# Output projection of a two-layer decoder trunk: attention rows by seven products on half blocks, norm scale applied after the product

## The chip, the cores and the metric

The kernel runs on one core of a Trainium2 chip. The metric is device time in microseconds (us), the median of several executions. The core's engines run side by side, each working off its own queue in order: TensorE (PE; its weight loads are listed as PEld), VectorE (DVE), ScalarE (ACT), GpSimd (POOL) and the queue that issues DMAs (SP). They wait for each other through semaphores.

## The reference

Two layers, 256 tokens, model width 1024, all float32. Each layer computes

```python
h = rms_norm(x, ln_w);  proj = h @ w_in
q, k, v, g, z, xbc, dt = split(proj)
attn = moba_attention(q, k, v) * silu(g)             # 256 x 1024
y = ssd_scan(silu(conv(xbc)), dt) * silu(z)          # 256 x 1024
y = rms_norm(y.reshape(256, 2, 512), ssd_norm_w)     # two groups of 512
x = x + concat([attn, y]) @ w_out                    # w_out: 2048 x 1024
```

The change concerns the last two lines: the group norm and the product with `w_out`.

## The kernel before

Every float32 operand of a large product is split into a high part (a float32r copy, made by ACT) and a low part (the operand minus that copy, made by DVE). A product is three matmuls: high x high, low x high and high x low, all added in the same PSUM bank.

The weights lie in DRAM in the order of use, in pieces of 128 x 1024 float32 (512 KB). `Weights.load` fetches a piece into one of four `raw` buffers; `Weights.pump` turns it into a pair `wh` (ACT, L101) and `wl` (DVE, L102). There are eight such pairs (`NB`): a piece can be split once the pair eight places earlier has been read for the last time by TensorE. The pieces of layer 0 carry numbers: 48 to 55 are the z projection, 56 to 63 the attention rows of `w_out` (`oa0`, `oa1`), 64 to 71 its SSD rows (`ob`, `oc`). Layer 1 repeats the pattern.

A layer runs through the projections v, q, k, x, g, z and then the output projection. In g the attention output is gated into `aT` and split into `ah` and `al` (L189). In z the SSD output `x2` is gated (L510, L663), and after each half `group_norm` follows: squares (ACT), a sum over channels (L519), a one-column matmul `np` for the sum over partitions, a power on POOL, two diagonal matrices `dg` (L532), two float32 matmuls `rg` against ones that spread the scale over partitions (L537), the scaling of `x2` (L540, four instructions) and its split into `sh` and `sl` (L188, L189).

The output projection keeps four PSUM banks, one for each half of the tokens (t) and each half of the columns (j), and adds all sixteen row blocks of `w_out` into them: eight from attention, then two and six from SSD. A bank is 16 x 3 matmuls of 512 columns. Its end is one DVE addition to the residual `x` (L698); in layer 0 it is followed by the first steps of the next layer's norm, in layer 1 by the store.

A generator that has to wait for another engine is put aside and resumed after a number of weight pieces (`yield 3`). The order of each engine's instructions is set by the Tile framework when the program is built: it follows the program text, and a modelled timeline decides which ready instruction goes first. On the chip each engine keeps this order.

Of the kernel before, what the change touches and what calls it, by code (L numbers as in the profile page):

```python
# [15 lines left out]
P = 128  # L16
S = 256
# [31 lines left out]
class Weights:  # L49


    def __init__(self, nc, raw_pool, wh_pool, wl_pool, w):
        self.nc, self.w = nc, w
        self.raw_pool, self.wh_pool, self.wl_pool = raw_pool, wh_pool, wl_pool
        self.loads, self.subs, self.index = [], [], {}
        off = NX
        for l in range(NL):
            for name, _, kt, wd in CHUNKS:
                self.index[(l, name)] = len(self.subs)
                for r in range(kt // KR):  # L60
# [4 lines left out]
        self.nload = 0  # L65
        self.raw = {}
# [17 lines left out]
    def steps(i):  # L84

        return [slice(k, k + 1) for k in range(KR)] if i == 0 else [slice(0, KR)]

    def pump(self, upto=None, before=None):
        nc = self.nc
        upto = len(self.subs) if upto is None else upto  # L90
        while self.prepped < upto and self.prepped - self.freed < NB:
            i = self.prepped
            li, s, wd = self.subs[i]
            self.load(li + RAWB - 1)
            src = self.raw[li]
            h = self.wh_pool.tile([P, KS, 512], F32R, tag="wh", name=f"wh{i}")
# [7 lines left out]
            self.parts[i] = (h, lo)  # L104
            if s == KR // KS - 1:
                del self.raw[li]
            self.prepped += 1
# [14 lines left out]
def hybrid_kernel(ctx: ExitStack, tc: tile.TileContext, x, par, w, out):  # L122
# [188 lines left out]
    def first_norm(rs, hT, lT):  # L311

        dg = tmp.tile([P, S], F32, tag="sr", name="dg0", bufs=1)
        for t in range(2):
            tl = slice(t * P, (t + 1) * P)
            dve.tensor_scalar(dg[:, tl], ident, rs[:, t:t + 1], None, ALU.mult)
        yield 3
        rg = bank("rg0")
# [193 lines left out]

    def group_norm(L, g, y, sh, sl):
        pc = L * NPAR
# [11 lines left out]
        dve.tensor_scalar(nv, np_[:, 0:2], 1.0 / 512.0, 4.0 * EPS, ALU.mult, ALU.add)  # L526
        rn = small.tile([P, 2], F32, tag="rn", name="rn")
        rpow(rn, nv)
        dg = tmp.tile([P, S], F32, tag="sr", name="dg", bufs=1)
        for t in range(2):  # L530
            ts = slice(t * P, (t + 1) * P)
            dve.tensor_scalar(dg[:, ts], ident, rn[:, t:t + 1], None, ALU.mult)  # L532
        yield 2
        rg = bank("rg")
        for t in range(2):
            ts = slice(t * P, (t + 1) * P)
            pe.matmul(rg[:, ts], ones, dg[:, ts], start=True, stop=True)  # L537
        for c in range(4):
            ct = 4 * g + c
            dve.scalar_tensor_tensor(y[:, ct, :], y[:, ct, :],  # L540
                                     par_sb[:, pc + C_SW + ct:pc + C_SW + ct + 1], rg[:, 0:256],
                                     ALU.mult, ALU.mult)
            if c % 2:
                split(sh[:, ct - 1:ct + 1, :], sl[:, ct - 1:ct + 1, :], y[:, ct - 1:ct + 1, :])

    hT = lT = None
    msum = [None, None]
    for L in range(NL):
# [16 lines left out]
        else:  # L565
            hv, lv = hT, lT
            resume(pre_norm(L, 1, hT, lT, msum[1], 4))

# [76 lines left out]

        ah = keep.tile([P, 8, S], F32R, tag="qT", name=f"ah{L}")
        al = keep.tile([P, 8, S], F32R, tag="kT", name=f"al{L}")
# [10 lines left out]
        sl = keep.tile([P, 8, S], F32R, tag="cb1", name=f"sl{L}")  # L658
        for pr in range(4):
            ps = ps_p.tile([P, 512], F32, tag="ps_p", name=f"z{pr}")  # L660
# [3 lines left out]
            if pr % 2 == 1:  # L664
                resume(group_norm(L, pr // 2, x2, sh, sl))


        po = {}

        def mm_out(name, t, j, lh, ll, start, stop):  # L670
            for i, (c, ps) in enumerate(po[t, j]):
                mm_tokens(L, name, (t,), lh, ll, (ps,), start, stop,
                          t == 1 and i == len(po[t, j]) - 1, c)

        for j in range(2):
            for t in range(2):
                po[t, j] = [((0, 512), ps_p.tile([P, 512], F32, tag="ps_p", name=f"o{t}{j}"))]
                if L == NL - 1 and t == j == 1:

                    po[t, j] = [((0, 256), po[t, j][0][1]), ((256, 512), bank("o11b"))]  # L680
                mm_out(f"oa{j}", t, j, ah, al, True, False)
        drain()
        for j in range(2):
            for t in range(2):
                mm_out(f"ob{j}", t, j, sh, sl, False, False)
        region = tc.manual_schedule(engines={mybir.EngineType.PE})
        for t in range(2):
            msum[t] = small.tile([P, 2], F32, tag="ms", name=f"ms{t}")
            if t == 1:
                region.__enter__()  # L690
            for j in range(2):
                for i, ((a, b), ps) in enumerate(po[t, j]):
                    mm_tokens(L, f"oc{j}", (t,), sh, sl, (ps,), False, True,
                              t == 1 and b == 512, (a, b))
                    cs = slice(j * 512 + a, j * 512 + b)
                    xs = x_sb[t][:, cs]
                    with urgent():
                        dve.tensor_tensor(xs, xs, ps[:, a:b], ALU.add)  # L698
                    if L == NL - 1:
                        nc.sync.dma_start(out[t * P:(t + 1) * P, cs], xs)  # L700
                if L < NL - 1:
# [10 lines left out]
def layout(inputs):  # L712
# [56 lines left out]
```

## Time and profile before

| | |
|---|---|
| median of 3 runs | 453.02 us (452.85 to 453.19) |
| the profiled execution | 452.3 us, span of its instructions 450.5 us |
| TensorE busy | 446.1 us, 99% of the span |
| VectorE busy | 346.7 us, 77% |
| ScalarE busy | 279.7 us, 62% |
| granted TensorE clock | 1.00 throughout |

TensorE is at work from the first microsecond to the last. A matmul's record is longer than the distance to the next one, because matmuls overlap in the array, so its cost here is the distance between the starts of two neighbours, not the length of a record. The same holds in small for DVE and ACT: neighbours overlap by about 0.08 us, and a group of n records gives the cost of one as the group's time over n.

### The profile page before, as it was taken

The numbers are of one execution on the slowest core, as the hardware profiler recorded it, in microseconds if no ns is written. First come the engines' busy times: TensorE is split into PE (matmuls) and PEld (weight loads), VectorE is DVE, ScalarE is ACT, GpSimd is POOL, SyncE is SP. The second block draws the span as 40 slices with busy tenths as digits, with TensorE's granted clock in tenths as the row PEclk, the third lists the DMA queues.
The fourth block names the chain that finished last, engine by engine and source line by source line (L and its number), as shares of the span: only waits on it lengthen the run. The fifth ranks groups of instructions, "written<-read, shape, count | busy, mean of one in ns | idle before, by whom it ended". The sixth has DMA issues, their size and how long they took to land.

```text
span 450.5 us, 7880 instructions
## 1 busy us (share of the span) xinstructions
PE 446.1 (99%) x2956; PEld 406.0 (90%) x2956; DVE 346.7 (77%) x636; ACT 279.7 (62%) x571; POOL 23.9 (5%) x29
## 2 busy tenths in 40 slices
PE   9999999999999999999999999999999999999997
PEld 9998878999999999888899878889999989998986
DVE  7597876799999888766565784686999999787621
ACT  7776779778558645534556656977657865555400
POOL 0000320200000000000000011110000000000000
PEclk9999999999999999999999999999999999999999
DMA  8888886452355155556246988561435444553301
GB/s 282 275 250 294 284 302 249 143 185 95 95 188 176 60 160 186 169 188 182 61 138 232 284 278 288 185 227 53 139 109 175 139 141 128 200 180 121 121 25 70
DMA packets 26373, 79.43 MB, mean 176 GB/s; under 512 B 2624, under 2 KB 9440, under 8 KB 25824
## 3 DMA queue, kind: packets, MB, share of 16 engines
q1 hardware_dynamic: 26048, 78.68, 53.3%
q8 instruction: 23, 0.38, 0.3%
q10 hardware_dynamic: 288, 0.27, 0.2%
q14 instruction: 14, 0.11, 0.1%
HBM read 77.85 MB, written 1.08 MB: 175 GB/s over the span
## 4 chain that ended last, share of the span: by engine, by line
PE 99%; DVE 0%; issue 0%
PE o L227 6%; PE o L226 6%; PE o L228 6%; PE xb L244 5%; PE xb L246 5%; PE xb L245 5%; PE z L245 3%; PE v L228 3%; PE z L244 3%; PE v L226 3%; PE v L227 3%; PE z L246 3%; PE k L227 3%; PE g L246 3%; PE g L244 3%; PE g L245 3%
## 5 line engine op out<-in xcount | busy, mean ns | idle before, releaser
L102 DVE TENSOR_TENSOR wl<-raw,wh 128x1024 fp32r<-128x1024 f32 (+3 forms) x145 | 166.0, 1157 | 41.3 <-ACT wh L101 40.1
L101 ACT CAST wh<-raw 128x1024 fp32r<-128x1024 f32 (+3 forms) x145 | 143.9, 999 | 59.8 <-DMA raw<-in_w_dram 15.9
L244 PE MATMUL xb<-hT,wh 128*128 128x256 f32 x192 | 56.3, 293 | 0.0
L245 PE MATMUL xb<-lT,wh 128*128 128x256 f32 x192 | 54.4, 283 | 0.0
L246 PE MATMUL xb<-hT,wl 128*128 128x256 f32 x192 | 53.9, 281 | 0.0
L245 PEld LDWEIGHTS xb<-lT,wh 128*128 128x128 f32 x192 | 36.2, 189 | 0.3
L246 PEld LDWEIGHTS xb<-hT,wl 128*128 128x128 f32 x192 | 36.2, 189 | 0.1
L244 PEld LDWEIGHTS xb<-hT,wh 128*128 128x128 f32 x192 | 36.2, 188 | 0.2
L246 PE MATMUL g<-hT,wl 128*128 128x256 f32 x128 | 36.3, 283 | 0.0
L245 PE MATMUL z<-lT,wh 128*128 128x256 f32 x128 | 36.2, 283 | 0.0
L244 PE MATMUL g<-hT,wh 128*128 128x256 f32 x128 | 36.1, 282 | 0.0
L244 PE MATMUL z<-hT,wh 128*128 128x256 f32 x128 | 36.0, 281 | 0.0
L245 PE MATMUL g<-lT,wh 128*128 128x256 f32 x128 | 35.9, 281 | 0.0
L246 PE MATMUL z<-hT,wl 128*128 128x256 f32 x128 | 35.9, 280 | 0.0
L447 DVE SCALAR_TENSOR_TENSOR cv<-rw,par_sb,cv 128x256 f32<-128x256 f32 x72 | 31.6, 481 | 4.2 <-ACT cv L444 4.2
L226 PE MATMUL k<-wh,hT 128*128 128x512 f32 x64 | 25.4, 397 | 0.0
L227 PE MATMUL k<-wh,lT 128*128 128x512 f32 x64 | 25.4, 397 | 0.0
L228 PE MATMUL k<-wl,hT 128*128 128x512 f32 x64 | 25.4, 397 | 0.0
L227 PE MATMUL q<-wh,lT 128*128 128x512 f32 x64 | 25.1, 394 | 0.0
L226 PE MATMUL q<-wh,hT 128*128 128x512 f32 x64 | 25.1, 394 | 0.0
L227 PE MATMUL o<-wh,al 128*128 128x512 f32 (+1 forms) x64 | 24.7, 386 | 0.0
L228 PE MATMUL q<-wl,hT 128*128 128x512 f32 x64 | 24.6, 395 | 0.0
(197 smaller groups left out, 1106.6 us busy)
## 6 DMA issues: line engine op xcount, KB each, us to landing
raw<-in_w_dram SPq DMA_DIRECT2D x120, 512.0 KB, 4.3
raw<-in_w_dram SPq DMA_DIRECT2D x15, 348.0 KB, 3.7
cb<-cd SPq DMA_DIRECT2D x4, 1024.0 KB, 7.8
raw<-in_w_dram SPq DMA_DIRECT2D x8, 344.0 KB, 3.6
x<-in_x_dram SPq DMA_DIRECT2D x2, 512.0 KB, 5.2
xT<-in_w_dram SPq DMA_DIRECT2D x3, 256.0 KB, 4.3
out_dram<-x SPq DMA_DIRECT2D x3, 256.0 KB, 2.0
raw<-in_w_dram SPq DMA_DIRECT2D x2, 174.0 KB, 3.2
```

What stands on the lines that cost most here:

```text
L101: nc.scalar.copy(h[:, ks, :wd], src[:, ks, :wd])
L102: nc.vector.tensor_tensor(lo[:, ks, :wd], src[:, ks, :wd], h[:, ks, :wd].bitcast(F32), ALU.subtract)
L226: pe.matmul(ps[:, cs], lh[:, kl, tl], wh[:, kk, cs], start=first, stop=False)
L227: pe.matmul(ps[:, cs], ll[:, kl, tl], wh[:, kk, cs], start=False, stop=False)
L228: pe.matmul(ps[:, cs], lh[:, kl, tl], wl[:, kk, cs], start=False, stop=final)
L244: pe.matmul(o, wh[:, kk, cs], lh[:, k, :], start=(k == 0 and c == 0), stop=False)
L245: pe.matmul(o, wh[:, kk, cs], ll[:, k, :], start=False, stop=False)
L246: pe.matmul(o, wl[:, kk, cs], lh[:, k, :], start=False, stop=(k == KT - 1 and c == 1))
L447: dve.scalar_tensor_tensor(cv[:, c, :], rw[:, c, k:k + S], cw(k), cv[:, c, :], ALU.mult, ALU.add)
```

## The change

**Seven products.** The attention part of the output projection is A times W for each half of the columns, with A 256 tokens x 1024 and W 1024 x 512. Both are cut into 2 x 2 blocks: A11, A12 (first 128 tokens; channels 0 to 511 and 512 to 1023), A21, A22 (last 128 tokens), and B11, B12, B21, B22 of 512 x 256. Eight block products become seven (Winograd's form of Strassen's scheme): S1 = A22 - A21, S3 = A11 - A21, S2 = A11 + S1, S4 = S2 - A12 on one side; T1 = B11 + B12, T2 = T1 + B22, T3 = B12 + B22, T4 = T2 + B21 on the other. The products are q5 = S1 T1, q1 = A11 B11, q6 = S2 T2, q7 = S3 T3, q4 = A22 T4, q2 = A12 B21, q3 = S4 B22, each 12 matmuls of 256 columns. The sums on the weight side are made in the kernel (`combine`, in place in the `raw` buffers and in a tile `t`), for both layers and both halves, and each of the seven operands is split into `wh` and `wl` as its own piece. The results are added to and subtracted from `x` piecewise, straight from PSUM, through a helper tile `uv`.

**Norm.** `group_norm` no longer spreads the scale over partitions. The SSD rows are multiplied by `ssd_norm_w` alone as they are split, and the per-token scale `rn` is applied when the result leaves PSUM. For that `ob` and `oc` are now one norm group each (four row blocks each), with a PSUM bank and an addition of their own.

In the changed kernel pieces 56 to 62 are the seven operands of `oa0`, 63 to 69 those of `oa1`, 70 to 73 are `ob` and 74 to 77 are `oc`.

```diff
-CHUNKS += [("ob%d" % i, 8, 2, 512) for i in range(2)]
-CHUNKS += [("oc%d" % i, 10, 6, 512) for i in range(2)]
+CHUNKS += [("ob%d" % i, 8, 4, 512) for i in range(2)]
+CHUNKS += [("oc%d" % i, 12, 4, 512) for i in range(2)]
+FAST = ("oa0", "oa1")
+FAST_SUBS = ("t1", "b11", "t2", "t3", "t4", "b21", "b22")
...
+    def combine(self, li, n):
+        add = self.nc.vector.tensor_tensor
+        b11, b12, b22, b21 = [self.raw.get(li + i) for i in range(4)]
+        if n == "t1":
+            self.t = self.keep.tile([P, KR, 512], F32, tag="bc", name=f"t{li}")
+            add(self.t, b11, b12, ALU.add)
+        elif n == "t2":
+            add(self.t, self.t, b22, ALU.add)
+        elif n == "t3":
+            add(b12, b12, b22, ALU.add)
+        elif n == "t4":
+            add(self.t, self.t, b21, ALU.add)
+        return {"b11": b11, "t3": b12, "b22": b22, "b21": b21}.get(n, self.t), \
+            {"b11": 0, "t3": 1, "b22": 2, "b21": 3}.get(n)
...
-            self.load(li + RAWB - 1)
-            src = self.raw[li]
+            self.load(self.used + RAWB - 1)
+            gone = 0
+            if isinstance(s, str):
+                src, gone = self.combine(li, s)
+            else:
+                src = self.raw[li]
...
 # group_norm
+        for ct in range(4 * g, 4 * g + 4):
+            sw = par_sb[:, pc + C_SW + ct:pc + C_SW + ct + 1]
+            act.activation(sh[:, ct, :], y[:, ct, :], AF.Copy, scale=sw)
+            dve.scalar_tensor_tensor(sl[:, ct, :], y[:, ct, :], sw, sh[:, ct, :].bitcast(F32),
+                                     ALU.mult, ALU.subtract)
...
-        dg = tmp.tile([P, S], F32, tag="sr", name="dg", bufs=1)
-        for t in range(2):
-            dve.tensor_scalar(dg[:, ts], ident, rn[:, t:t + 1], None, ALU.mult)
-        yield 2
-        rg = bank("rg")
-        for t in range(2):
-            pe.matmul(rg[:, ts], ones, dg[:, ts], start=True, stop=True)
-        for c in range(4):
-            dve.scalar_tensor_tensor(y[:, ct, :], y[:, ct, :], ..., rg[:, 0:256],
-                                     ALU.mult, ALU.mult)
-            if c % 2:
-                split(sh[:, ct - 1:ct + 1, :], sl[:, ct - 1:ct + 1, :], y[:, ct - 1:ct + 1, :])
...
-            split(ah[:, hs, :], al[:, hs, :], aT[:, hs, :])
+            if pr == 1:
+                part("a11", a11)
+        part("a22", a22)
+        dve.tensor_tensor(a22, a22, a21, ALU.subtract)
+        part("s1", a22)
+        dve.tensor_tensor(a21, a11, a21, ALU.subtract)
+        part("s3", a21)
+        dve.tensor_tensor(a11, a11, a22, ALU.add)
+        part("s2", a11)
+        part("a12", a12)
+        dve.tensor_tensor(a12, a11, a12, ALU.subtract)
+        part("s4", a12)
...
+        def out_part(name, t, j, lh, ll, rn, cuts=((0, 512),)):
+            for i, (a, b) in enumerate(cuts):
+                ps = ps_p.tile([P, 512], F32, tag="ps_p", name=f"{name}{t}")
+                mm_tokens(L, f"{name}{j}", (t,), lh, ll, (ps,), True, True, ..., (a, b))
+                with urgent():
+                    dve.scalar_tensor_tensor(xs, ps[:, a:b], rn[:, t:t + 1], xs,
+                                             ALU.mult, ALU.add)
...
+        def out_fast(j):
+            for i, (n, a) in enumerate((("q5", "s1"), ("q1", "a11"), ("q6", "s2"), ("q7", "s3"),
+                                        ("q4", "a22"), ("q2", "a12"), ("q3", "s4"))):
+                ws.pump()
+                if i % 2 == 0:
+                    ps = ps_p.tile([P, 512], F32, tag="ps_p", name=f"f{L}{j}{i}")
+                q[n] = ps[:, i % 2 * S:(i % 2 + 1) * S]
+                ah, al = fast[a]
+                for k in range(4):
+                    pe.matmul(q[n], ah[:, k, :], wh[:, k, :], start=(k == 0), stop=False)
+                    pe.matmul(q[n], al[:, k, :], wh[:, k, :], start=False, stop=False)
+                    pe.matmul(q[n], ah[:, k, :], wl[:, k, :], start=False, stop=(k == 3))
+                ws.free(i0 + i)
+                with urgent():
+                    if n == "q1":
+                        act.copy(uv[:, 0, :], q["q1"])
+                        dve.tensor_tensor(x1[0], x1[0], q["q1"], ALU.add)
+                    elif n == "q6":
+                        dve.tensor_tensor(uv[:, 0, :], q["q6"], uv[:, 0, :], ALU.subtract)
+                        dve.tensor_tensor(uv[:, 1, :], uv[:, 0, :], q["q5"], ALU.subtract)
+                        dve.tensor_tensor(x1[1], x1[1], uv[:, 1, :], ALU.add)
+                        dve.tensor_tensor(x2[1], x2[1], uv[:, 1, :], ALU.add)
...                 # q7: three, q4, q2, q3: one each
         for j in range(2):
-                mm_out(f"oa{j}", t, j, ah, al, True, False)
+            out_fast(j)
         drain()
-        for j in range(2):
-            for t in range(2):
-                mm_out(f"ob{j}", t, j, sh, sl, False, False)
+        for t in range(2):
+            out_part("ob", t, 0, sh, sl, rns[0])
...             # then for each t: ob of j = 1, oc of both j
```

The rest of the diff changes a wait by one piece in `first_norm` and in `pre_norm`, and lays out the blocks of `w_out` in DRAM.

Three places show how the engines' queues change in layer 0. The first is DVE near the end of the z projection. Names: `x2*g2z` rows gate z, `wl60` is the low part of weight piece 60, `sr` is the norm's sum. Before:

```order
L510 SCALAR_TENSOR_TENSOR g2z_2243<-thz_2241,z2_2176 128x512
L663 TENSOR_TENSOR x2_0_967<-x2_0_967,g2z_2243 128x512
L102 TENSOR_TENSOR wl60_2273<-raw60_2131,wh60_2272 128x1024
L102 TENSOR_TENSOR wl61_2291<-raw61_2149,wh61_2290 128x1024
L526 TENSOR_SCALAR nv_2222<-np_2219 128x2
L102 TENSOR_TENSOR wl62_2309<-raw62_2177,wh62_2308 128x1024
L532 TENSOR_SCALAR dg_2226<-ident_124,rn_2224 128x128 x2
L102 TENSOR_TENSOR wl63_2337<-raw63_2270,wh63_2336 128x1024
L510 SCALAR_TENSOR_TENSOR g2z_2326<-thz_2324,z3_2246 128x512
L663 TENSOR_TENSOR x2_0_967<-x2_0_967,g2z_2326 128x512
```

After:

```order
L711 TENSOR_TENSOR x2_0_967<-x2_0_967,g2z_2261 128x512
L543 SCALAR_TENSOR_TENSOR g2z_2330<-thz_2328,z3_2264 128x512
L133 TENSOR_TENSOR wl60_2281<-t56_2128,wh60_2280 128x1024
L700 TENSOR_TENSOR aT0_731<-aT0_731 128x4x128
L133 TENSOR_TENSOR wl61_2297<-raw59_2126,wh61_2296 128x1024
L566 TENSOR_SCALAR nv_2244<-np_2241 128x2
L133 TENSOR_TENSOR wl62_2313<-raw58_2054,wh62_2312 128x1024
L222 TENSOR_TENSOR f20_1726<-aT0_731,f20_1726 128x4x128
L759 TENSOR_TENSOR x0_84<-x0_84,f000_2356 128x256
L711 TENSOR_TENSOR x2_0_967<-x2_0_967,g2z_2330 128x512
L558 SCALAR_TENSOR_TENSOR sl0_2052<-x2_0_967,par_sb_86,sh0_2051 128x256 x2
L105 TENSOR_TENSOR t60_2350<-raw60_2162,raw61_2277 128x1024
```

Between the gating of z2 and that of z3 (`L663` before, `L711` after) there stood four splits of weights with the norm's `nv` and `dg`; now there stand three splits, a subtraction on `aT`, the low part of an A operand and the first addition from a product.

The second place is DVE in the first half of the attention part. Names: `f000` holds q5 and q1 of column half 0, `f002` q6 and q7, `f004` q4 and q2, `f006` q3; `t60` is the weight sum of column half 1. Before:

```order
L519 TENSOR_REDUCE sr_2331<-ysq_2329 128x256
L102 TENSOR_TENSOR wl64_2395<-raw64_2288,wh64_2394 128x1024
L189 TENSOR_TENSOR sl0_2039<-x2_0_967,sh0_2038 128x512 x2
L102 TENSOR_TENSOR wl65_2407<-raw65_2306,wh65_2406 128x1024
L102 TENSOR_TENSOR wl66_2419<-raw66_2334,wh66_2418 128x1024
L102 TENSOR_TENSOR wl67_2432<-raw67_2392,wh67_2431 128x1024
L526 TENSOR_SCALAR nv_2361<-np_2358 128x2
L532 TENSOR_SCALAR dg_2365<-ident_124,rn_2363 128x128 x2
```

After:

```order
L109 TENSOR_TENSOR raw61_2277<-raw61_2277,raw62_2346 128x1024
L133 TENSOR_TENSOR wl63_2353<-t60_2350,wh63_2352 128x1024
L133 TENSOR_TENSOR wl64_2370<-raw60_2162,wh64_2369 128x1024
L762 TENSOR_TENSOR uv_2385<-uv_2385,f000_2356 128x256
L566 TENSOR_SCALAR nv_2411<-np_2408 128x2
L107 TENSOR_TENSOR t60_2350<-t60_2350,raw62_2346 128x1024
L763 TENSOR_TENSOR x0_84<-x0_84,uv_2385 128x256
L764 TENSOR_TENSOR x1_85<-x1_85,uv_2385 128x256
L766 TENSOR_TENSOR uv_2385<-uv_2385,f002_2395 128x256
L774 TENSOR_TENSOR x0_84<-x0_84,f006_2480 128x256
L767 TENSOR_TENSOR x1_85<-x1_85,f002_2395 128x256
L768 TENSOR_TENSOR x1_85<-x1_85,uv_2385 128x256
```

Before, four of the eight rows split weights; now two of twelve do, and the others add blocks of weights or move products from PSUM into `x` and `uv`.

The third place is TensorE. Before, at the first `rg`:

```order
L227 MATMUL o00_2333<-wh59_2179,al0_1725 128x512
L228 MATMUL o00_2333<-wl59_2180,ah0_1724 128x512
L226 MATMUL o10_2374<-wh56_2115,ah0_1724 128x512
L537 MATMUL rg_2259<-dg_2226,ones_103 128x128 x2
L227 MATMUL o10_2374<-wh56_2115,al0_1725 128x512
L228 MATMUL o10_2374<-wl56_2116,ah0_1724 128x512
```

After, at the end of column half 1 (`wh69`, q3) where the SSD rows begin (`ob`):

```order
L748 MATMUL f016_2625<-wh69_2476,f300_1727 128x256
L749 MATMUL f016_2625<-wh69_2476,f310_1728 128x256
L259 MATMUL ob0_2639<-wh70_2498,sh0_2051 128x512
L260 MATMUL ob0_2639<-wh70_2498,sl0_2052 128x512
L259 MATMUL ob1_2659<-wh70_2498,sh0_2051 128x512
L260 MATMUL ob1_2659<-wh70_2498,sl0_2052 128x512
L750 MATMUL f016_2625<-wl69_2477,f300_1727 128x256
L748 MATMUL f016_2625<-wh69_2476,f300_1727 128x256
```

The `rg` matmuls are gone, and four matmuls of `ob` that need only `wh70` stand ahead of the first matmul that reads `wl69`.

## Rows read from the trace of the kernel before

**Rows 1.** Page: span, busy time, share, instructions of each engine.
```profile
span 450.5 us, 7880 instructions
...
PE 446.1 (99%) x2956; PEld 406.0 (90%) x2956; DVE 346.7 (77%) x636; ACT 279.7 (62%) x571; POOL 23.9 (5%) x29
```

**Rows 2.** Page: the chain that ended last, by engine.
```profile
PE 99%; DVE 0%; issue 0%
```

**Rows 3.** Timeline of TensorE: start us, us, engine line op out<-in; z, layer 0.
```profile
166.80 0.28 PE L244 MATMUL z<-hT,wh 128*128 128x256 f32 x1
...
178.46 0.28 PE L244 MATMUL z<-hT,wh 128*128 128x256 f32 x1
```

**Rows 4.** Timeline of TensorE, output projection of layer 0, its end, and layer 1's last.
```profile
180.68 0.40 PE L226 MATMUL o<-wh,ah 128*128 128x512 f32 x1
...
184.18 0.40 PE L226 MATMUL o<-wh,ah 128*128 128x512 f32 x1
...
227.02 0.32 PE L226 MATMUL v<-wh,hT 128*128 128x348 f32 x1
...
446.89 0.28 PE L228 MATMUL o11b<-wl,sh 128*128 128x256 f32 x1
```

**Rows 5.** Chain in order of time, layer 0: start us, us, what.
```profile
186.67 0.44 PE rg L537 x4
...
222.18 0.87 PE tp L277 x8
```

**Rows 6.** Timeline of DVE, layer 0, and one row of layer 1.
```profile
161.27 0.68 DVE L510 SCALAR_TENSOR_TENSOR g2z<-thz,g 128x512 f32<-128x512 f32 x1
161.87 0.68 DVE L189 TENSOR_TENSOR al<-aT,ah 128x512 fp32r<-128x512 f32 x1
...
171.60 0.68 DVE L510 SCALAR_TENSOR_TENSOR g2z<-thz,z 128x512 f32<-128x512 f32 x1
172.31 0.69 DVE L663 TENSOR_TENSOR x<-x,g2z 128x512 f32<-128x512 f32 x1
...
187.16 1.65 DVE L540 SCALAR_TENSOR_TENSOR x<-x,par_sb,rg 128x256 f32<-128x256 f32 x4 [2.65 <-PE rg L537]
188.73 2.03 DVE L519 TENSOR_REDUCE sr<-ysq 128x256 f32<-128x1024 f32 x1
...
191.81 1.29 DVE L189 TENSOR_TENSOR sl<-x,sh 128x512 fp32r<-128x512 f32 x2
193.01 3.49 DVE L102 TENSOR_TENSOR wl<-raw,wh 128x1024 fp32r<-128x1024 f32 x3
...
221.04 0.48 DVE L267 TENSOR_SCALAR hn<-x,rs 128x512 f32<-128x512 f32 x1
...
445.09 0.42 DVE L698 TENSOR_TENSOR x<-x,o 128x256 f32<-128x256 f32 x1 [1.43 <-PE o L228]
```

**Rows 7.** Timeline of ACT: first tanh of z in each layer, a weight copy.
```profile
163.53 0.60 ACT L508 ACTIVATE thz<-z 128x512 f32<-128x512 f32 x1 [5.29 <-PE z L246]
164.76 1.05 ACT L101 CAST wh<-raw 128x1024 fp32r<-128x1024 f32 x1 [0.63 <-PE z L245]
...
384.10 0.60 ACT L508 ACTIVATE thz<-z 128x512 f32<-128x512 f32 x1 [5.35 <-PE z L246]
```

**Rows 8.** Stretches: us, PE, PEld, DVE, ACT, POOL busy (instructions), clock, DMA.
```profile
160.70:180.70 20.00, 20.00 (x173) 19.80 (x170) 17.10 (x23) 10.54 (x12) 0.70 (x1) 1.00 0.55 189
180.70:227.02 46.32, 46.32 (x214) 38.25 (x213) 30.85 (x45) 21.96 (x32) 1.25 (x2) 1.00 0.50 147
```

**Rows 9.** Page: DMA issues, KB each, us to landing; and throughput in 40 slices.
```profile
GB/s 282 275 250 294 284 302 249 143 185 95 95 188 176 60 160 186 169 188 182 61 138 232 284 278 288 185 227 53 139 109 175 139 141 128 200 180 121 121 25 70
...
raw<-in_w_dram SPq DMA_DIRECT2D x120, 512.0 KB, 4.3
```

**Rows 10.** Page: granted clock in 40 slices; chain: the warm-up matmuls at the start.
```profile
PEclk9999999999999999999999999999999999999999
...
1.05 5.97 PE warm L165 x28
```

More of the change, by code (lines that the diff above doesn't have):

```diff
@@ L59, in __init__ @@
                 self.index[(l, name)] = len(self.subs)
+                if name in FAST:
+                    self.subs += [(len(self.loads), n, 512) for n in FAST_SUBS]
+                    for _ in range(4):
+                        self.loads.append((off, 512))
+                        off += P * KR * 512
+                    continue
                 for r in range(kt // KR):
@@ L104, in pump @@
             self.parts[i] = (h, lo)
-            if s == KR // KS - 1:
-                del self.raw[li]
+            if gone is not None:
+                del self.raw[li + gone]
+                while self.used < self.nload and self.used not in self.raw:
+                    self.used += 1
             self.prepped += 1
@@ L643, in hybrid_kernel, with part @@
                 resume(ssd_quarter(L, pr, x2, dth, ac, nac, cb, cms[pr // 2], dsh))
-        ah = keep.tile([P, 8, S], F32R, tag="qT", name=f"ah{L}")
-        al = keep.tile([P, 8, S], F32R, tag="kT", name=f"al{L}")
+        fh = keep.tile([P, 4, 4, P], F32R, tag="qT", name=f"fh{L}")
+        fl = keep.tile([P, 4, 4, P], F32R, tag="kT", name=f"fl{L}")
+        f2 = keep.tile([P, 2, 4, 2, P], F32R, tag="v", name=f"f2{L}")
+        f3 = [keep.tile([P, 4, P], F32R, tag="ehi", name=f"f3{i}{L}", bufs=2) for i in range(2)]
+        fast = {}
+        homes = [(fh[:, i], fl[:, i]) for i in range(4)]
+        homes += [(f2[:, i, :, 0, :], f2[:, i, :, 1, :]) for i in range(2)] + [(f3[0], f3[1])]
+        lo_k, hi_k, lo_t, hi_t = slice(0, 4), slice(4, 8), slice(0, P), slice(P, S)
+        a11, a12 = aT[:, lo_k, lo_t], aT[:, hi_k, lo_t]
+        a21, a22 = aT[:, lo_k, hi_t], aT[:, hi_k, hi_t]
+        def part(n, src):
+            fast[n] = homes[len(fast)]
+            split(*fast[n], src)
         for pr in range(4):
@@ L664, in hybrid_kernel @@
             if pr % 2 == 1:
[L665 to L673, printed above, removed]
-        for j in range(2):
-            for t in range(2):
-                po[t, j] = [((0, 512), ps_p.tile([P, 512], F32, tag="ps_p", name=f"o{t}{j}"))]
-                if L == NL - 1 and t == j == 1:
-                    po[t, j] = [((0, 256), po[t, j][0][1]), ((256, 512), bank("o11b"))]
-                mm_out(f"oa{j}", t, j, ah, al, True, False)
+                rns.append(small.tile([P, 2], F32, tag=f"rn{pr // 2}", name="rn", bufs=1))
@@ new lines, in hybrid_kernel @@
+                resume(group_norm(L, pr // 2, x2, sh, sl, rns[-1]))
+        def out_part(name, t, j, lh, ll, rn, cuts=((0, 512),)):
+            for i, (a, b) in enumerate(cuts):
+                ps = ps_p.tile([P, 512], F32, tag="ps_p", name=f"{name}{t}")
+                mm_tokens(L, f"{name}{j}", (t,), lh, ll, (ps,), True, True,
+                          t == 1 and i == len(cuts) - 1, (a, b))
+                cs = slice(j * 512 + a, j * 512 + b)
+                xs = x_sb[t][:, cs]
+                with urgent():
+                    if rn is None:
+                        dve.tensor_tensor(xs, xs, ps[:, a:b], ALU.add)
+                    else:
+                        dve.scalar_tensor_tensor(xs, ps[:, a:b], rn[:, t:t + 1], xs,
+                                                 ALU.mult, ALU.add)
+                if name == "oc" and L == NL - 1:
+                    nc.sync.dma_start(out[t * P:(t + 1) * P, cs], xs)
@@ L690, in hybrid_kernel @@
                 region.__enter__()
+            out_part("ob", t, 1, sh, sl, rns[0])
             for j in range(2):
[L692 to L700, printed above, removed]
+                out_part("oc", t, j, sh, sl, rns[1],
+                         ((0, 256), (256, 512)) if L == NL - 1 and t == j == 1 else ((0, 512),))
                 if L < NL - 1:
@@ L730, in layout @@
                 src = wi[:, c0:c0 + wd]
+            if name in FAST:
+                for r, c in ((0, 0), (0, 1), (1, 1), (1, 0)):
+                    b = src[r * 512:(r + 1) * 512, c * S:(c + 1) * S]
+                    ws.append(b.reshape(4, P, S).transpose(1, 0, 2).reshape(-1))
+                continue
             ws.append(src.reshape(kt // KR, KR, P, wd).transpose(0, 2, 1, 3).reshape(-1))
```

39 lines of the change are left out of this document (26 added, 13 removed).

## The prediction

> **What bounds the kernel now.** I read the page's busy times first: TensorE is at work for 446.1 of 450.5 us [rows 1], and the chain that ended last is PE for 99% [rows 2]. So time that leaves TensorE's queue is gained, and work on another engine costs nothing as long as TensorE never waits for it. The second question is how much room the other engines have, and a mean over the span doesn't tell: DVE is busy 77% [rows 1], but in the 20 us before the output projection it is busy 17.1 of 20.0, and in the output projection 30.9 of 46.3 [rows 8]. The room lies behind the place where the change puts its DVE work.
>
> **The change on TensorE.** Neighbouring 256-column matmuls start 0.1178 us apart: 99 of them from 166.80 to 178.46 [rows 3]. 512-column ones start 0.2333 apart: 15 from 180.68 to 184.18 [rows 4]. The attention part of a layer is 4 banks x 8 blocks x 3 = 96 matmuls of 512, 22.4 us. After the change it is 2 halves x 7 products x 12 = 168 of 256, 19.8 us. Each needs its own weight load, but so do those of z, so the price is taken from z. Gain 2.6 us a layer. The `rg` matmuls go: 0.44 [rows 5], twice a layer, 0.9 us. The SSD part keeps its 96 matmuls. Two layers: 7.0 us off TensorE, if nothing waits. The two changed waits in `first_norm` and `pre_norm` move a few matmuls by one weight piece inside stretches without idle time; I cost them at nothing. `rn` now has to be there only when `ob` leaves PSUM, over 20 us after `np`.
>
> **The change on DVE.** Prices from rows 6, as group time over count with the overlap of about 0.08 taken off: a 128x1024 tensor-tensor 1.14 (three in 3.49), 128x512 0.60 (two in 1.29; 161.27 to 161.87), a 128x256 scalar-tensor-tensor 0.39 (four in 1.65), a 128x256 addition from PSUM 0.42 alone (445.09), 0.34 without its end, which I take; with dependent neighbours 0.11 comes on top (171.60 to 172.31 is 0.71 where 0.60 is the price), so 0.53 from above. Additions of weight blocks are not in this trace; the nearest is the split itself, same shape, type and operand count: 1.14. From below I bound them by the one-operand row at 221.04, 0.40 for 512 elements, so 0.80. Per layer:
> - 6 more splits (14 pieces instead of 8) and 8 additions of weights: 14 x 1.14 = 16.0
> - 7 low parts of A operands and 4 sums, for 4 `al`: +7 x 0.60 = 4.2
> - 22 additions from products at 0.34 = 7.5, and 4 more at the end of `ob`, 2.4
> - norm: 8 scalings (L540) turn into 8 scaled low parts, 4 low parts of 128x512 and 4 `dg` go: about -3.2
>
> Net +27 us on DVE in the 67 us from 160 to 227, in which it now idles 18 (20.0 - 17.1 and 46.3 - 30.9 [rows 8]). That sum alone says that the cover is gone. ACT gets six more copies, seven A casts for four and eight more small ones, about 9 us, and has room for that: 10.5 of 20.0 and 22.0 of 46.3 busy [rows 8].
>
> **Where TensorE waits.** I followed DVE's new order in layer 0 from a point where both orders agree: the gating of g3, at 161.27 before [rows 6], 0.60 earlier now since one `al` less stands ahead, so 160.67. From there through `wl69` (the last operand of column half 1) DVE has, in the order that stands there: 14 splits 16.0, 8 weight additions 9.1, 6 low parts and 4 sums for A 6.0, ten 128x512 gatings 6.0, 10 small scalar-tensor-tensors (`yp`, `sl`) 3.9, two reduces at 1.95 together 3.9, 0.3 of tiny ones, 18 additions from products 6.1. Sum 51.2 us, so 211.9, and 212.2 with 0.3 of waits for ACT at the start. From 166 on nothing in the list waits: the results of TensorE that it reads are there before it comes to them.
>
> TensorE enters the attention part at 180.5 (z0 ends at 163.53 [rows 7], 144 more matmuls of z at 0.1178). Unhindered, it would want `wl69` after 12 more products of 1.41 and one `np` (0.3), at 197.7. It gets it 14.5 us later. The eight pairs are a lead of 8 x 1.41 = 11 us of TensorE time only, and DVE needs over 3 us for a piece with its addition and its share of the `x` updates. The stalls come in pieces, by the same walk: about 0.9 at 183.5 (high part of S2), 2.2 at 186.5 (low part of S2, behind seven DVE rows), 2.2 at 190.0 (S4), the rest before `wl63`, `wl65`, `wl67` and `wl68`/`wl69`. The order lets four `ob` matmuls run ahead (0.9 us).
>
> After `wl69`: 10 matmuls of q3 end at 213.4; `wl70` comes two DVE rows later (0.34 + 1.14), 213.7; 20 matmuls of `ob` x 0.2333 = 4.7, then q2 1.4: 219.8; 72 left at 0.2333 = 16.8 and `tp` 0.87 [rows 5]: 237.5.
>
> A new wait follows on SP: four `raw` buffers now hold one half's four blocks until its last operand is split, so `ob`'s and `oc`'s six pieces can be fetched only from 212.2 on. A piece lands 4.3 us after its issue [rows 9], the next ones 1.8 apart (512 KB at the 290 GB/s of the fastest slices [rows 9]): 216.5 to 225.5. Cast (1.05 less the overlap [rows 7]) and split take 2.1 more: the last is ready at 227.6, and TensorE, at 1.4 us a piece from 219.8, wants its low part at 227.3. I take 0.5 us in all; from below 0, from above 3 (the landings less hidden). End of layer 0's projection: 238.0, against 227.02 before [rows 4]: +11.0.
>
> Layer 1 has the same list and the same distances: 238.0 - 163.53 - 0.87 (no `tp`) = 73.6 from the end of z0, against 447.0 - 384.1 = 62.9 before [rows 4, 7]: +10.7. The store at the end is unchanged.
>
> Sum: 452.3 (the profiled execution: its span of 450.5 and 1.8 around it) + 21.7 = 474.0. The median of the runs lies 0.7 above that execution, so 475.
>
> **The rivals.**
> 1. *The lead is enough.* The eight pairs and the idle DVE time of the projection take up the extra work, and TensorE's saving is the result: 452.3 - 7.0 = 445.3, 446 as a median. For it: TensorE is 99% of the chain and DVE 77% of the span. Against it: DVE would have to do 51.2 us of work between 160.67 and 197.7, which is 37. It decides if these rows cost 28% less than here.
> 2. *DVE is cheaper, but not cheap enough.* Weight additions at 0.80, nothing lost to DMA: 2 x (8 x 0.34 + 0.5) = 6.4 less, 468.
> 3. *TensorE's clock falls.* The granted clock is full in every slice of the trace, with no stall in it [rows 10]; what stalls of 1 to 3 us do, no row shows. The one price for slow matmuls is the warm-up: 28 records in 5.97 us, 0.213 for 128 columns in two passes [rows 10] against 0.11 for the `rg` ones [rows 5], though its clock reads full too. At twice the distance the attention part is 39.6 us instead of the 33 between 180.5 and 213.4: +6 a layer, 487. The Trainium skill (TensorE: Matmul & The Clock Gate, section Part 1: The HAM clock gate) states the rule behind this rival: the array runs at half rate by default and goes back to it after idling. The attention part would be the first stretch in which TensorE idles a third of the time; no run here has tried it.
> 4. *Buffers.* `raw62` is fetched only after `wl62` (188.1) and lands at 192.4, 3 us before the addition that reads it. Should landing take twice as long, both halves wait: up to 3 us a layer, 481.
>
> **Chances.** Forecast with its neighbours 2 and 4: 0.82 (2 alone 0.12, 4 alone 0.08). Clock: 0.09. Rival 1: 0.06. Left for a balance near zero: 0.03. A run tells 0.2% (0.9 us) from no change: slower 0.92, within 0.02, faster 0.06. The range goes from rival 2 with the product additions a quarter cheaper too (36 x 0.08 = 3: 465) to product additions at 0.53 (36 x 0.19 = 6.8) and 2.5 us a layer more of waits for DMA (5): 487.
>
> **What would show it.** Right: TensorE idle for 12 to 15 us a layer between the first product and `ob`, in pieces of 1 to 3 us, released by DVE at the low parts of weights and A operands; DVE without idle time from about 166 to 215; then short waits of ACT for `raw`; 256-column matmuls of the products at 0.118. Wrong: idle DVE in that stretch; a weight addition well under 1.1 us; a granted clock under 1.00 there; or TensorE's idle time behind DMA instead of DVE.

## The result and the profile after

The changed kernel takes 477.22 us (median of four runs, 476.41 to 477.53) against 452.94 for the kernel before: a ratio of 1.053, 95% interval 1.051 to 1.055. The profiled execution took 477.5, with a span of 475.7. The forecast was 475.0, in a range of 465 to 487.

The page after: the busy line, the chain by engine, the granted clock in 40 slices. They answer to [rows 1, 2, 10].

```profile
PE 452.9 (95%) x3048; PEld 416.1 (87%) x3048; DVE 399.1 (84%) x714; ACT 297.0 (62%) x601; POOL 29.4 (6%) x29
...
PEclk9999999999999999799999999999999999987999
...
PE 65%; DVE 21%; DMA 6%; issue 4%; ACT 2%; SPq 1%; POOL 1%; DVEq 0%; ACTq 0%; POOLq 0%
```

TensorE has fallen from 99% of the chain to 65%; DVE holds 21% where it held nothing. By the two stretches of [rows 8], with the same columns, the loss lies in the second:

```profile
160.70:180.70 20.00, 20.00 (x172) 19.41 (x171) 19.35 (x28) 10.40 (x16) 0.00 (x0) 1.00 0.33 110
180.70:227.02 46.32, 38.41 (x244) 34.72 (x243) 44.95 (x64) 22.21 (x28) 4.50 (x2) 0.93 0.41 130
```

DVE is busy for 44.95 of 46.32 us (30.85 before), TensorE only for 38.41. The timeline of TensorE in the seven products of layer 0, cut to the rows with idle time ahead of them (in brackets: idle us and who ended it):

```profile
187.58 0.39 PE L748 MATMUL f<-wh,f 128*128 128x256 f32 x1 [0.87 <-ACT f L221]
...
191.61 0.39 PE L749 MATMUL f<-wh,f 128*128 128x256 f32 x1 [1.90 <-DVE f L222]
...
195.07 0.58 PE L749 MATMUL f<-wh,f 128*128 128x256 f32 x1 [1.20 <-DVE f L222]
...
201.92 0.36 PE L748 MATMUL f<-wh,fh 128*128 128x256 f32 x1 [1.64 <-DVE nv L566]
...
206.17 0.38 PE L750 MATMUL f<-wl,f 128*128 128x256 f32 x1 [0.90 <-DVE wl L133]
...
209.53 0.36 PE L748 MATMUL f<-wh,fh 128*128 128x256 f32 x1 [0.47 <-DVE uv L761]
...
212.03 0.39 PE L750 MATMUL f<-wl,fh 128*128 128x256 f32 x1 [0.60 <-DVE wl L133]
...
214.96 0.39 PE L750 MATMUL f<-wl,f 128*128 128x256 f32 x1 [0.31 <-DVE wl L133]
```

The first three are the forecast's stalls at S2 (high, then low part) and S4: 0.9, 2.2 and 2.2 were forecast. The wait at 201.92 is put down to `nv`, a row of two columns; what ended just before it on DVE is L762, the last reader of a product in a bank (201.37 to 201.78), and that bank is wanted next. So TensorE waits for two kinds of things: operands, and banks that DVE has still to read.

The timeline of DVE from the point at which the forecast's walk began to `wl69` (x2: `wl68` and `wl69`), which answers to 161.27 and 193.01 in [rows 6], with the idle times in brackets at either end:

```profile
163.00 0.68 DVE L543 SCALAR_TENSOR_TENSOR g2z<-thz,g 128x512 f32<-128x512 f32 x1
...
166.93 0.69 DVE L543 SCALAR_TENSOR_TENSOR g2z<-thz,z 128x512 f32<-128x512 f32 x1 [0.65 <-ACT thz L541]
...
172.75 1.22 DVE L107 TENSOR_TENSOR t<-t,raw 128x1024 f32<-128x1024 f32 x1
173.89 0.68 DVE L543 SCALAR_TENSOR_TENSOR g2z<-thz,z 128x512 f32<-128x512 f32 x1
...
201.37 0.41 DVE L762 TENSOR_TENSOR uv<-uv,f 128x256 f32<-128x256 f32 x1
201.70 0.14 DVE L566 TENSOR_SCALAR nv<-np 128x2 f32<-128x2 f32 x1
...
212.55 2.36 DVE L133 TENSOR_TENSOR wl<-raw,wh 128x1024 fp32r<-128x1024 f32 x2
...
218.36 1.23 DVE L133 TENSOR_TENSOR wl<-raw,wh 128x1024 fp32r<-128x1024 f32 x1 [0.18 <-ACT wh L132]
```

From 163.00 to 214.83 are 51.8 us; the sum was 51.2, and 51.5 with the waits for ACT. Between the two idle times DVE has no pause. An addition of weight blocks takes 1.14 up to its neighbour's start, an addition from a product 0.33.

The granted clock did fall, too. Windows of layer 0, columns as in [rows 8]:

```profile
190.00:192.00 2.00, 0.39 (x3) 0.40 (x4) 2.00 (x4) 0.00 (x0) 2.00 (x1) 1.00 0.60 170
192.00:194.00 2.00, 1.87 (x10) 1.58 (x9) 2.00 (x4) 1.42 (x3) 0.11 (x1) 0.54 0.90 260
194.00:196.00 2.00, 0.93 (x4) 0.93 (x5) 2.00 (x3) 1.99 (x4) 0.00 (x0) 0.50 0.23 94
196.00:198.00 2.00, 2.00 (x12) 2.00 (x10) 2.00 (x5) 0.44 (x1) 0.00 (x0) 0.50 0.00 0
198.00:200.00 2.00, 2.00 (x14) 2.00 (x14) 2.00 (x3) 0.00 (x0) 0.00 (x0) 0.75 0.00 0
200.00:202.00 2.00, 0.36 (x4) 0.19 (x3) 2.00 (x5) 0.00 (x0) 0.07 (x1) 1.00 0.00 0
```

After the 1.90 us standstill it is at 0.50 (1.2 GHz; the values between are means over a change), and at 1.00 (2.4 GHz) again by 200. TensorE then waits 1.64 us for DVE, which works without a pause, so in this stretch the slow matmuls cost nothing that the wait wouldn't have cost.

The ends for [rows 4]: the output projection of layer 0 begins, layer 1 begins, its output projection begins, and the last matmul. Then the start of layer 1's output projection in the kernel before.

```profile
183.32 0.28 PE L748 MATMUL f<-wh,fh 128*128 128x256 f32 x1
...
240.50 0.32 PE L259 MATMUL v<-wh,hT 128*128 128x348 f32 x1
...
415.71 0.28 PE L748 MATMUL f<-wh,fh 128*128 128x256 f32 x1
...
472.04 0.28 PE L261 MATMUL oc<-wl,sh 128*128 128x256 f32 x1
```

```profile
401.25 0.40 PE L226 MATMUL o<-wh,ah 128*128 128x512 f32 x1
```

Layer 0's output projection starts at 183.32 (180.68 before) and lasts 57.18 us instead of 46.34: +10.84. Layer 1's, from 415.71, lasts 56.33 instead of 45.64: +10.69. Of the 25.15 us between the two last matmuls, 3.6 lie outside, in stages that the change doesn't touch. The timeline shows one place: the z matmuls, first and last of 167 without a gap, stand 0.1199 apart; 0.1178 in [rows 3].

```profile
163.29 0.28 PE L278 MATMUL z<-lT,wh 128*128 128x256 f32 x1
...
183.20 0.28 PE L279 MATMUL z<-hT,wl 128*128 128x256 f32 x1
```

### The profile page after: what moved, and what is told of

It reads as the page before. It is cut to its first block, busy times and chain, and to the rows that moved or that the text cites. A ratio compares the mean times of both kernels' runs of the same rounds, so it can differ in the third digit from the quotient of the medians.

```text
span 475.7 us, 8188 instructions
## 1 busy us (share of the span) xinstructions
PE 452.9 (95%) x3048; PEld 416.1 (87%) x3048; DVE 399.1 (84%) x714; ACT 297.0 (62%) x601; POOL 29.4 (6%) x29
## 4 chain that ended last, share of the span: by engine, by line
PE 65%; DVE 21%; DMA 6%; issue 4%; ACT 2%; SPq 1%; POOL 1%; DVEq 0%; ACTq 0%; POOLq 0%
DVE wl L133 7%; DMA raw<-in_w_dram 5%; PE xb L279 4%; PE xb L278 4%; PE xb L277 4%; PE g L277 3%; PE g L279 3%; PE g L278 3%; PE q L259 3%; PE q L260 3%; PE q L261 3%; PE yp L531 2%; PE k L260 2%; PE k L259 2%; PE k L261 2%
## 5 line engine op out<-in xcount | busy, mean ns | idle before, releaser
L132 ACT CAST wh<-t 128x1024 fp32r<-128x1024 f32 x12 | 12.6, 1049 | 24.9 <-DVE t L107 16.5
L218 POOL TENSOR_TENSOR rr<-se,mhalf 128x4 f32<-128x4 f32 x16 | 19.0, 1188 | 119.0 <-DVE se L377 86.6
```

The costliest lines, as they stand in the source:

```text
L132: nc.scalar.copy(h[:, ks, :wd], src[:, ks, :wd])
L218: pool.tensor_tensor(o, i, mhalf[:, :n], ALU.pow)
```

## The experiments

The kernel before, run beside them, took 452.9 to 453.3. "The stretch" is layer 0's output projection, first matmul to the start of layer 1: 46.3 before, 57.2 after.

**Where the other 3.6 us come from: the place of the weight tiles.** The two `rn` buffers need 64 bytes less than the four before, and `raw`, `wh` and `wl` lie 64 bytes lower in each partition. The first run puts them back, the second shifts the kernel before.

```diff
+    small.tile([P, 16], F32, tag="pad", name="pad", bufs=1)     # e1, changed kernel
-        rn = small.tile([P, 2], F32, tag="rn", name="rn")       # e2, kernel before
+        rn = small.tile([P, 2], F32, tag="rn", name="rn", bufs=2)
```

> The changed kernel with one unused tile of 64 bytes per partition added to the pool of small tiles, so that raw, wh and wl lie again at the addresses of the kernel before (wh from byte 162752 of a partition instead of 162688). The order of no engine is meant to change. Theory 1 (the place of wh and wl in SBUF sets the distance of the 256-column matmuls): 0.1198 us apart in x, g and z falls back to about 0.116, 0.1198 - 0.116 = 0.0035 x 672 x 2 = 4.7 us less, the 512-column ones give about 1 us back: 473.6 us. Rival (the distance follows from the program's order or the load of the other engines): 477.2 and 0.1198 as before.

> The kernel before with two buffers less for the tile rn, nothing else: raw, wh and wl move 64 bytes down, to the addresses of the changed kernel. Theory 1 (place in SBUF): 256-column matmuls 0.1198 apart instead of 0.116, 512-column ones 0.228 instead of 0.230: 453.0 + 3.6 = 456.5 us. Rival: 453.0 and no change in the distances.

Measured: 474.51 (ratio 1.047, 1.045 to 1.049) and 456.36 (1.0065, 1.005 to 1.008). So the place is worth 2.7 us in the one, where 3.6 were expected, and about 3 in the other, where 3.5 were. The instructions of every engine stand in the same order with and without the shift, in both pairs, so it isn't the order. Of the 3.6 us about 1 is left that isn't traced. The same two rows of z in the padded kernel, again the ends of 167, are 0.1177 apart:

```profile
162.46 0.28 PE L279 MATMUL z<-lT,wh 128*128 128x256 f32 x1
...
182.00 0.28 PE L280 MATMUL z<-hT,wl 128*128 128x256 f32 x1
```

From the first `xb` matmul of layer 0 to its output projection the kernels take 101.6 (before) and 101.2 (padded) at the old place, 103.9 (after) and 104.7 (e2) at the low one.

**The norm part alone**, with eight products, padded.

```diff
-FAST = ("oa0", "oa1")
+FAST = ()
...
-            out_fast(j)
+            for t in range(2):
+                out_part("oa", t, j, ah, al, None)
```

> Only the second part of the change: the norm's scale at evacuation and ob/oc as one norm group each, with the attention rows by eight products as before (in banks of their own, added to x when they leave PSUM), wh and wl at the addresses of the kernel before. Theory A (TensorE's work counts as long as DVE keeps up): the rg matmuls go, 4 x 0.44 = 1.8 us, and DVE has about 1.6 us more a layer, which is covered: 451.2 us, no waits of TensorE. Rival B (the norm part brings waits too, for banks or for rn): 453 or more, with TensorE idle in the output projection.

Measured: 451.28 (0.995, 0.9935 to 0.997), as expected. The stretch is 45.55. Of the kernels here that leave nothing out, it is the only one that beats the one before.

**Taking DVE's new work away, piece by piece.** e4 splits plain blocks (no pad, so 477.2 is its base); e5 leaves the products unread; e7 does both.

```diff
-            add(self.t, self.t, b22, ALU.add)      # e4, e7: all four additions of a half
-                with urgent():                     # e5, e7: all updates of x from products
-                    ...
```

> The changed kernel without the sixteen additions of weight blocks: the seven operands are raw blocks (T1 = B11, T2 and T3 = B12, T4 = B22), so the attention rows of the output are not the reference's. Everything else stays. DVE loses 9.1 us a layer, and its order now has wl69 ahead of most updates of x: about 34 us of work up to it instead of 51.2, where TensorE wants it after 37. Theory A (TensorE waits for DVE's sum of work): hardly any waits, 477.2 - 10.8 - 10.7 - 7.0 = 449 us, up to 453 with what is left. Rival C (TensorE waits for banks, that is for the updates of x, or for its own lower clock): not more than the 18 us of DVE work that is left out and probably half of it, 459 to 468 us.

> The changed kernel with the 64-byte pad, without the 22 additions (and 2 copies) that take the seven products of each column half into x: the products are computed and not read, so the output lacks the attention part. The 8 additions of weight blocks a layer stay. Theory (one queue): only DVE's sum up to the last weight piece counts; it falls by 18 x 0.34 = 6.1 us a layer from 51.2, so the end of each output projection comes 6.1 earlier: 474.5 - 12.2 = 462, and TensorE's waits in the products are for weight pieces alone. Rival (two separate deadlines: weight pieces and the return of product banks, each of which alone is enough to delay TensorE, as the run without weight additions suggests, which gained 4.7 and 5.0 a layer instead of 9.1): with the updates gone, weight pieces still stand where they stood in DVE's order and the gain is under 4 a layer: 467 to 472.

> The changed kernel with the 64-byte pad, without the 8 additions of weight blocks a layer (operands are plain blocks) and without the 22 additions of the products into x: the output is not that of the layer. All 168 small matmuls, 14 splits and the A operands stay. Theory (DVE's queue is the whole loss): DVE's sum up to the last weight piece is 51.2 - 9.1 - 6.1 = 36.0, done at 196.7 where TensorE wants it at 197.7; TensorE's saving of 3.5 a layer is left, less at most 3 a layer for the transfers of ob's pieces that wait for buffers: 447 to 453. Rival (something else than DVE's queue is in the way as well: the buffers, the clock, the small matmuls' own distance): 456 or more.

Measured: 470.18 (1.037, 1.034 to 1.039), 466.10 (1.029, 1.028 to 1.030) and 446.11 (0.985, 0.984 to 0.986). The gains are 7.0 and 8.4 alone, against 474.5 with the pad 28.4 together. In e4 the theory failed, and the time lies above the rival's range (459 to 468) too; e5 lies between its two theories, and e7 0.9 below its range. One kind of work less doesn't shorten the stretch by its own sum. e7 shows why the forecast held all the same: without both, the stretch is 43.57, TensorE is 99% busy, its clock stays full in all 40 slices, and the time is that of rival 1, 446. The small matmuls, the splits, the buffers and the transfers, which e7 keeps, cost nothing of themselves; what it leaves out, DVE's additions (with two small copies of ACT a layer), is the whole loss. Its page:

```profile
PE 439.3 (99%) x3048; PEld 406.1 (91%) x3048; DVE 366.7 (83%) x654; ACT 296.1 (67%) x597; POOL 33.2 (7%) x29
```

What TensorE waited for in e4 (waits: engine, line, releaser, us in total, times, longest):

```profile
PE f L739 <- DVE uv L753: 4.2, 2, 2.4
PE f L739 <- DVE uv L752: 4.1, 2, 2.0
PE f L739 <- DVE x L765: 1.4, 2, 1.3
```

None of these is a weight; all are banks: the updates of x, which stand in DVE's order between the splits, are a second deadline.

**Does the clock eat the gain?** In e4, 33 matmuls of layer 0 stand 0.21 apart after a standstill, which would be 3 us. e9 (from e4) and e10 (from e1) compute two products a layer twice, to fill waits of TensorE. DVE does the same work in both pairs, but not row for row in the same order, as the expectations have it: a dozen of its 698 rows in e9 and eight of 714 in e10 stand some places earlier or later.

```diff
+                twice = j == 0 and n in ("q3", "q7")
-                for k in range(4):
+                for k in [0, 1, 2, 3] * (1 + twice):
```

> The kernel without weight additions (its output is not the reference's), with two products a layer (q3 and q7 of column half 0) computed twice into the same bank, the second overwriting the first: 24 more small matmuls a layer on TensorE, 2.9 us, placed where it stood still before and where the granted clock then fell to 0.5. DVE's order is the same row for row. Theory (DVE's order alone decides; the half-speed stretch from 194 to 204 lies inside DVE's time, since the next product waits for a bank that DVE returns at 204.3): 470, at most 471, though TensorE does 5.8 us more. Rival (the clock's fall is what ate the gain of that run: 48 matmuls at 0.213 instead of 0.120, 4.5 us a layer, and a TensorE that doesn't stand still keeps it): 461 to 464. If TensorE's own work counted: 476.

> The changed kernel with the 64-byte pad, with the same two products a layer computed twice (2.9 us more of TensorE a layer, the same output). DVE's order is the same row for row. Theory (DVE's order decides): the additional matmuls go into waits of TensorE, 474.5, up to 476 where the clock is low while they run. Rival (the clock's fall to 0.5 costs what it shows, about 3 us a layer, and would go with the standstill): 468 to 471. If TensorE's own work counted: 480.

Measured: 471.38 (1.040, 1.038 to 1.041) and 475.18 (1.048, 1.0465 to 1.050): 1.2 and 0.7 more for 5.8 us more of TensorE, neither clear of the spread of the runs, and e9 0.4 above the 471 that was allowed. Two windows of e4, then of e9:

```profile
194.00:198.00 4.00, 2.44 (x12) 2.14 (x11) 4.00 (x6) 1.74 (x2) 0.00 (x0) 0.51 0.38 131
198.00:202.00 4.00, 3.81 (x18) 3.85 (x19) 4.00 (x6) 2.11 (x4) 0.00 (x0) 0.50 0.71 242
```

```profile
194.00:198.00 4.00, 3.83 (x32) 3.66 (x32) 4.00 (x6) 2.80 (x4) 0.00 (x0) 1.00 0.41 135
198.00:202.00 4.00, 2.03 (x17) 1.85 (x16) 4.00 (x7) 2.37 (x3) 0.00 (x0) 1.00 0.40 131
```

The clock is now full there, and TensorE waits instead: the next product starts at 203.91 (204.44 in e4), when DVE has read a bank. In e4:

```profile
203.88 0.42 DVE L765 TENSOR_TENSOR x<-x,f 128x256 f32<-128x256 f32 x1
```

In e9, TensorE's timeline:

```profile
203.91 0.36 PE L740 MATMUL f<-wh,f 128*128 128x256 f32 x1 [3.88 <-DVE x L766]
```

The bank that is waited for lets the next product start 21.1 us behind the first one in both kernels, at either clock. So in e4 the slow clock was shadow time: time in which TensorE would have waited anyway. (In e9 the clock falls later instead, at 204.21, for 3.41 us; in e4 it is low for 10.24.) e10 says less. There the clock still falls, at 191.66 and for 6.83 us, as it does in e1 (193.25, 6.83). A window of e10:

```profile
192.00:198.00 6.00, 4.27 (x20) 4.27 (x21) 6.00 (x8) 3.09 (x5) 0.00 (x0) 0.50 0.16 65
```

So e10 shows that 2.9 us more of TensorE a layer fit into its waits, and doesn't test the clock. For layer 0 of the changed kernel the shadow follows from DVE's timeline above: DVE doesn't pause from 166.93 to 218.18, so a faster TensorE would only have waited longer for it.

**Additions on GpSimd**, nothing left out.

```diff
-        add = self.nc.vector.tensor_tensor
+        add = self.nc.gpsimd.tensor_tensor
```

> The changed kernel with the 64-byte pad and the 8 additions of weight blocks a layer on GpSimd instead of VectorE; nothing left out. Theory (the additions cost by DVE's queue time): DVE loses the same 9.1 us a layer as in the run without additions, which was 4.7 and 5.0 a layer faster, so 474.5 - 9.7 = 465 if GpSimd needs no more than 3 us for one; 470 if it needs up to 5. Rival (GpSimd's additions slow DVE down, or come later than DVE would have had them): 474.5 or more.

Measured: 477.85 (1.055, 1.053 to 1.056), 3.3 us slower than on VectorE: the rival. One addition takes 2.4 to 5.1 us there (groups of GpSimd: busy us, mean ns, the groups of `t4` and `t2`, four rows each):

```profile
L111 POOL TENSOR_TENSOR t<-t,raw 128x1024 f32<-128x1024 f32 x4 | 17.7, 4421 | 23.2 <-DVE nv L567 13.3 <-DVE wl L133 9.9
...
L107 POOL TENSOR_TENSOR t<-t,raw 128x1024 f32<-128x1024 f32 x4 | 11.5, 2863 | 10.7 <-DVE wl L133 10.7
```

And DVE can be held up meanwhile. The addition at 197.51 on GpSimd lasts 2.40; on DVE's timeline the second of two equal splits falls beside it and takes 3.30 instead of 1.21:

```profile
196.22 1.21 DVE L133 TENSOR_TENSOR wl<-t,wh 128x1024 fp32r<-128x1024 f32 x1
197.35 0.41 DVE L763 TENSOR_TENSOR uv<-uv,f 128x256 f32<-128x256 f32 x1
197.68 3.30 DVE L133 TENSOR_TENSOR wl<-raw,wh 128x1024 fp32r<-128x1024 f32 x1
```

Against the same rows of the padded kernel (e1), six DVE rows of layer 0 and five of layer 1 last longer here, by 10.7 and 8.8 us in all: what DVE saved in additions, 9.1 a layer, it gave back. It isn't so beside every addition: two splits from 187.90 to 190.26 keep their usual 2.36, and the addition beside them takes 4.47.

**Seven products for the second half of the columns only**, with the norm part.

```diff
+FAST = ("oa1",)
...
+        for t in range(2):
+            out_part("oa", t, 0, ah, al, None)
+        split(*fast["s4"], a12)
+        out_fast(1)
```

> The norm part, and seven products for column half 1 alone (half 0 keeps eight), 64-byte pad, nothing left out. TensorE: 48 matmuls at 0.2333 turn into 84 at 0.1165, 1.4 us a layer less than with the norm part alone. DVE: 3 more splits, 4 additions of weights, 4 sums and 4 low parts of A operands, 11 product additions for 2 evacuations: 15 us a layer more, but the last weight piece is wanted only after eight long products and six short ones, at 200.2 by the clock of layer 0, and DVE's sum up to it is 37.0 from 161.3, so 198.3. Theory (a deadline, not a share): no wait, 451.3 - 2.8 = 448.5, up to 451 with waits for the transfers of ob's pieces. Rival (15 us more on DVE is too much wherever it stands): 453 or more.

Measured: 455.45 (1.005, 1.004 to 1.0065): slower, the rival's number. The expectation's sum was wrong twice. Up to the last weight piece DVE needed 41.6 us (162.43 to 204.04) instead of 37.0, since the sum had left rows out and 1.1 us of waits for ACT at the start; and it did not ask when banks come back, which bites first. TensorE's timeline at the one long stall of layer 0, up to the end of the slow matmuls:

```profile
197.10 0.50 PE L564 MATMUL np<-ones,sr 128*128 128x1 f32 x4
199.41 0.35 PE L746 MATMUL f<-wh,f 128*128 128x256 f32 x1 [1.81 <-DVE nv L567]
...
202.85 0.41 PE L748 MATMUL f<-wl,ah 128*128 128x256 f32 x1
203.07 0.35 PE L746 MATMUL f<-wh,ah 128*128 128x256 f32 x1
```

q7 goes to the second half of the bank that holds q6, and DVE reads q6 only at 198.85 to 199.26, behind a 2 us reduce and an addition of weights:

```profile
198.85 0.41 DVE L759 TENSOR_TENSOR uv<-f,uv 128x256 f32<-128x256 f32 x1
```

The granted clock falls to 0.50 in 200 to 202, 15 matmuls stand 0.21 apart (1.4 us), and this time nothing is late behind them, since TensorE's next wait is at 225.00 (0.27 us): here the clock is paid. The stretch is 48.7; 44.2 was hoped for. Stall and clock are 3.2 of these 4.5; the rest I have not traced. Layer 1 loses without a fall of the clock: its output projection takes 46.75 (44.62 in e3).

**Other places for the weight tiles**, in the norm-only kernel: pads of 128 and of 192 bytes, so 64 and 128 above the place of before. Every engine's order is that of e3.

> The kernel with the norm part alone (eight products), all weight tiles another 64 bytes higher in SBUF: 128 above the place that the changed kernel had, 64 above that of the kernel before. If only the low place is bad: 451.3, the same as without. If the cost changes with every step of 64 bytes and the place of before is the good one: 454 to 455. If higher is better still: 449 or less.

> The kernel with the norm part alone (eight products), all weight tiles 128 bytes higher in SBUF than in the kernel before. Measured so far: 64 below and 64 above that place cost 3 to 5 us. If the cost repeats every 128 bytes: 451.3, as with the place of before. If the place of before is a single good one: 455 to 457.

Measured: 456.72 (1.009, 1.007 to 1.011) and 454.72 (1.003, 1.002 to 1.0045), against 451.28 at the old place: the first above every number that was expected, the second just under the 455 to 457 of a single good place. Neither "lower is bad" nor a period of 128 bytes fits. Why a place is good stays open.

**All of them at a glance** (medians, us; stretch of layer 0 from the profiled run, which in e4 is the fastest of its four, 468.3).

| kernel | time | stretch |
|---|---|---|
| before | 452.9 | 46.3 |
| after / e1, padded | 477.2 / 474.5 | 57.2 / 57.4 |
| e3, norm part | 451.3 | 45.6 |
| e4, no weight additions (low place) | 470.2 | 52.5 |
| e5, no updates of x | 466.1 | 54.2 |
| e7, neither | 446.1 | 43.6 |
| e9, e4 with 48 more matmuls | 471.4 | 54.0 |
| e10, e1 with 48 more matmuls | 475.2 | 57.8 |
| e6, additions on GpSimd | 477.9 | 59.3 |
| e12, one half | 455.5 | 48.7 |

## Why the prediction was right

- **DVE's walk.** 51.2 us were summed, 51.8 came; the prices of the additions (1.14 and 0.34) came as 1.14 and 0.33. DVE's busy time rose by 52.4 us; twice 27 were forecast. The output projections were to end 11.0 and 10.7 us later by this walk; they last 10.84 and 10.69 longer. (Layer 0's ends 13.48 later, since it also begins 2.64 later.) e7 confirms the cause: without the additions of weights and products the loss is gone, and rival 1's 446 is what is left.
- **The pieces of the wait.** The first three stalls are right in cause and nearly in size (4.0 in all; 5.3 forecast); the waits in layer 0 add up to 7.9 us instead of the 12 to 15 that were to show it; over 2 us of the difference passed in slow matmuls, and the rest isn't traced. That the wait at 201.92 is for a bank, I had not separated: the forecast speaks of weights and A operands alone. It didn't matter for the sum, because both stand in one queue that hardly idles from 166.9 to 218; it did matter in e4 and e12, where I had thinned the queue for one deadline only.
- **TensorE's own gain** of 3.5 us a layer was to show in the rest of the projection. With DVE's work gone the stretch is 43.57, 2.8 below before, and layer 1's is 42.54, 3.1 below; e7 as a whole is 6.9 below the kernel before (453.05 beside it); 7.0 was the forecast's gain.
- **Rival 3, the clock.** It fell, as rival 3 had it, from 1.00 to 0.50 after the 1.90 us wait; a clock under 1.00 was one of the forecast's own signs of being wrong. The rule in the Trainium skill (TensorE: Matmul & The Clock Gate, section Part 1: The HAM clock gate) has it fall for an engine that goes idle, and the trace agrees. But the price of +6 a layer was wrong: with DVE busy without a pause, and by e9, it lies in DVE's shadow, about zero.
- **Rivals 2 and 4.** DVE's rows were not cheaper. The transfers of `ob`'s pieces leave three short gaps on DVE after 218 (0.18, 1.14, 0.86) and no wait on TensorE.
- **What was missed:** the place of the weight tiles, 2.7 us. It is more than the whole distance from 475.0 to 477.2; with the tiles at the old place (e1, 474.5) the forecast is half a microsecond too high.

## What to carry to other kernels

Trading matmuls for elementwise work is decided by a walk through the elementwise engine's queue against the time at which TensorE wants each result, both operands and banks to write into; busy shares don't tell (DVE is at 83% in e7, which is fast, and at 84% in the changed kernel). When one kind of late work is taken out, the other deadline keeps most of the loss, so list all of them before thinning the queue for one. And a change that resizes any buffer moves its neighbours: compare an untouched stage before explaining small differences by the change.

## What was not expected of the hardware

- 64 bytes of SBUF address of the weight tiles change the distance of 256-column matmuls from 0.1178 to 0.1199 us (z) and the whole kernel by 3 us (e1, e2); 64 and 128 bytes in the other direction cost 5.4 and 3.4 (e8, e11).
- A float32 addition of 128x1024 takes 1.14 us on VectorE and 2.4 to 5.1 on GpSimd; a VectorE split beside one took 3.30 instead of 1.21, and VectorE's rows lost as much, 10.7 and 8.8 us a layer, as the additions had cost it, 9.1 (e6).
- Useless matmuls in waits cost nearly nothing: 5.8 us of them moved the time by 0.7 and 1.2 (e9, e10).
